# Half of an MLP's second product by seven block products instead of eight, interleaved with the next eighth's first product (fp32 decoder trunk, one core)

## The chip, the cores and the metric

The kernel runs on one core of a Trainium2 chip. The metric is the device time of one execution in microseconds; lower is better. A core has five engines with a queue each: TensorE (PE: matmuls, and the loads of the stationary operand, listed as PEld), VectorE (DVE), ScalarE (ACT), GpSimd (POOL) and SyncE (SP), which issues the loads from memory here. An engine takes the instructions of its queue in order, and waits for other engines by semaphores.

## The reference

Two layers on x of 256 tokens by 2048, in float32: a recurrent block (RG-LRU) and an attention block, each followed by an MLP, with RMS norms before each and one at the end. What matters here is the MLP:

```python
def _mlp(h, w1, w2):
    u = jnp.einsum('bsd,df->bsf', h, w1)      # 2048 -> 8192
    u = jnp.square(jax.nn.relu(u))
    return jnp.einsum('bsf,fd->bsd', u, w2)   # 8192 -> 2048
...
    x = x + _mlp(_rmsnorm(x, mlp_norm[i]), mlp_w1[i], mlp_w2[i])
```

## The kernel before

**Precision.** Every product of float32 numbers is made of three matmuls on rounded operands (type fp32r). A value v is split into hi, its rounding, and lo = v - hi; hi x hi, hi x lo and lo x hi are summed in PSUM, and lo x lo is left out. For weights ScalarE makes hi (`cut_hi`, L86) and VectorE makes lo (`cut_lo`, L90).

**Units.** All weights come in units of 128x2048 (1 MB). SyncE loads a unit into one of three `raw` tiles (L76); ScalarE writes `whi` (four tiles), VectorE `wlo` (three tiles); then TensorE uses both. `before_unit(i)` (L103) is called ahead of unit i's matmuls. It issues the loads up to unit i+5, hi up to i+3 and lo up to i+2. Instructions stand in each engine's queue in the order in which this code issues them. Functions that `after(n, ...)` puts off (evictions, sums) are issued behind the matmuls of the item n places later.

**A unit of the first product** (x W1) holds 128 columns of W1 over all 16 blocks of 128 inputs. Weights are stationary, x is moving: `xT` holds per input block 256 columns of hi and 256 of lo, one per token. Per block that is hi of the weights with x-hi and x-lo, and lo of the weights with x-hi: 768 columns. `stand_w2` (L252) issues them in an order named by a style. The three "thirds" styles (`thirds`, `thirds_low_first`) use three matmuls of 256 columns into one sum, 48 a unit. The others take hi over 512 columns at once, 32 matmuls a unit, and add the two halves later (`tensor_reduce`, L493). Each quarter of an MLP has its own style (L702, L709): `thirds`, `wide_first`, `pairs`, `apart` in the first MLP; `thirds_low_first`, `fours`, `thirds`, `as_was` in the second. `u_done` (L488) then makes relu, scaling and square, and splits the result into a tile `aT` of 128 hidden features by 256 tokens (hi and lo). It has one VectorE instruction or two on PSUM (L491, or L493 and L494), two on ScalarE (L496, L498) and one on VectorE (L502).

**A unit of the second product** holds 512 rows of W2 (four blocks of 128) by 512 output columns. Here `aT` is stationary, 128 tokens of it at a time, and the weights are moving. `stand_x` (L265) issues per block and per half t of the tokens three matmuls of 512 columns, 24 a unit, into two PSUM banks, one per half of the tokens.

**Order of the MLP** (`plan_mlp`, L504). There are four quarters of 2048 hidden features. Each quarter has 16 first units, then 16 second units: four output chunks n of 512 columns, four units each; then `add_x` (L290) adds the two banks to the residual `xc[n]` (L292). At the start of an MLP two first units are taken in two parts, since the last input chunk is still being transposed. The end of the second MLP is `final_items` (L671). It runs the last chunk's last three units for tokens 0 to 127 first, and then for tokens 128 to 255; `final_rows` (L654) normalises and stores each half.

**The other products** (L216 `stand_w` for the recurrent block, in the order hi, hi, lo of 256 columns each; `stand_x` for the rest) use the same units and buffers.

## Time and profile before

| | us |
|---|---|
| median of 3 runs | 2199.34 |
| lowest, highest | 2195.87, 2200.32 |
| the profiled execution's own time | 2199.65 |
| span in its profile (first to last instruction) | 2197.9 |
| TensorE busy | 2175.3 |
| VectorE busy | 1280.0 |
| ScalarE busy | 1061.3 |

The recurrent layer takes the first 384 us or so, the first MLP runs to 1094, the attention to 1483 and the second MLP to the end. The profile gives, per group of instructions, its line, engine, operation, the tiles that it writes and reads, its count, the busy time and the mean duration of one. The chain that ended last follows the end of the program back through what released each step. TensorE's durations overlap, since matmuls are pipelined, so its pace is read from the starts of matmuls. Where two rows of a timeline on VectorE or ScalarE overlap by some hundredths, the second began before the first had written its last result.

### The profile page before, as it was taken

To read this page: it belongs to the slowest core of one execution; us is meant where nothing else is said; L and a number is where in the kernel's file an instruction comes from. 1 tells how busy PE (TensorE), PEld (TensorE's weight loads), DVE (VectorE), ACT (ScalarE), POOL (GpSimd) and SP (SyncE) were. 2 spreads that over 40 slices of the span, in tenths; PEclk is the share of its full clock that TensorE was granted. 3 is DMA by queue.
4 is the path that set the end of the run, shared out by engine and by line. 5 is a ranking of instruction groups with operands and counts; after the bars stand their busy time and mean duration, and the time that the engine had idled before them with its cause. 6 is when DMAs were issued, how large, how long until landed. Compare 5 with 4: busy or idle time off the path is not lost.

```text
span 2197.9 us, 29494 instructions
## 1 busy us (share of the span) xinstructions
PE 2175.3 (99%) x12490; PEld 1910.4 (87%) x12490; DVE 1280.0 (58%) x1344; ACT 1061.3 (48%) x1163; POOL 78.3 (4%) x42
## 2 busy tenths in 40 slices
PE   7999999999999999999999999999999999999998
PEld 7999988998888888888888888889988889988886
DVE  8898855554564565565555555555546645545654
ACT  5787754543443343344445544555434434433442
POOL 2221100000000000000000000000000000000001
PEclk9999999999999999999999999999999999999999
DMA  6565555455555555555554445455555555555553
GB/s 219 211 211 194 194 207 189 175 192 191 191 183 201 185 188 197 189 189 194 181 192 166 159 174 183 161 188 199 200 195 181 198 196 184 186 193 189 191 192 115
DMA packets 61700, 413.40 MB, mean 188 GB/s; under 512 B 6784, under 2 KB 7168, under 8 KB 13440
## 3 DMA queue, kind: packets, MB, share of 16 engines
q1 hardware_dynamic: 61568, 411.51, 53.3%
q8 instruction: 98, 1.61, 0.3%
q14 instruction: 34, 0.28, 0.0%
HBM read 409.39 MB, written 2.10 MB: 187 GB/s over the span
## 4 chain that ended last, share of the span: by engine, by line
PE 96%; DVE 2%; ACT 1%; POOL 0%; DMA 0%; issue 0%; SPq 0%; DVEq 0%; ACTq 0%
PE acc L142 93%; PE g L142 1%; DVE wlo L90 1%; PE tr L176 0%; PE tr L568 0%; PE g L576 0%; DMA xg<-in_xT 0%; DVE xT L750 0%; PE tr L599 0%; POOL a L357 0%; ACT whi L86 0%; POOL c L358 0%; PE g L609 0%; PE g L608 0%; PE g L607 0%
## 5 line engine op out<-in xcount | busy, mean ns | idle before, releaser
L90 DVE TENSOR_TENSOR wlo<-raw,whi 128x2048 fp32r<-128x2048 f32 (+3 forms) x400 | 883.4, 2212 | 345.6 <-PE acc L142 267.9
L86 ACT ACTIVATE whi<-raw 128x2048 fp32r<-128x2048 f32 (+3 forms) x400 | 736.8, 1844 | 525.2 <-PE acc L142 437.6
L142 PE MATMUL acc<-xT,whi 128*128 128x256 f32 (+1 forms) x4064 | 882.7, 317 | 7.0 <-ACT whi L86 6.3
L142 PE MATMUL acc<-whi,aT 128*128 128x512 f32 x2624 | 813.9, 390 | 0.0
L142 PEld LDWEIGHTS acc<-xT,whi 128*128 128x128 f32 x4064 | 653.8, 190 | 46.4 <-ACT whi L86 6.7
L142 PE MATMUL acc<-xT,wlo 128*128 128x256 f32 x2672 | 654.9, 280 | 7.1 <-DVE wlo L90 6.8
L142 PEld LDWEIGHTS acc<-whi,aT 128*128 128x128 f32 x2624 | 492.6, 188 | 102.2
L142 PE MATMUL acc<-wlo,aT 128*128 128x512 f32 x1312 | 510.7, 389 | 0.0
L142 PEld LDWEIGHTS acc<-xT,wlo 128*128 128x128 f32 x2672 | 481.8, 190 | 27.6 <-DVE wlo L90 8.3
L142 PEld LDWEIGHTS acc<-wlo,aT 128*128 128x128 f32 x1312 | 246.3, 188 | 50.5
L142 PE MATMUL acc<-whi,xT 128*128 128x512 f32 x768 | 245.9, 395 | 0.0
L496 ACT ACTIVATE mu<-mr 128x256 f32<-128x256 f32 x128 | 53.5, 418 | 370.2 <-DVE mr L494 242.7
L142 PEld LDWEIGHTS acc<-whi,xT 128*128 128x128 f32 x768 | 144.3, 188 | 30.7
L142 PE MATMUL acc<-wlo,xT 128*128 128x512 f32 x384 | 150.4, 392 | 0.0
L493 DVE TENSOR_REDUCE mr<-acc 128x256 f32<-128x512 f32 x80 | 55.3, 692 | 156.1 <-PE acc L142 156.1
L292 DVE TENSOR_TENSOR xc<-xc,acc 128x512 f32<-128x512 f32 x78 | 53.2, 687 | 97.7 <-PE acc L142 97.7
L491 DVE SCALAR_TENSOR_TENSOR mr<-acc,rstdB 128x256 f32<-128x256 f32 x48 | 20.2, 424 | 112.9 <-PE acc L142 112.9
L142 PEld LDWEIGHTS acc<-wlo,xT 128*128 128x128 f32 x384 | 72.2, 188 | 15.1
L643 POOL TENSOR_TENSOR xc<-xc,gB 128x1024 f32<-128x1024 f32 x3 | 10.6, 3534 | 1879.9 <-DMA raw<-in_w 1843.4
L498 ACT ACTIVATE aT<-mu 128x256 fp32r<-128x256 f32 x128 | 53.6, 419 | 4.1
L502 DVE TENSOR_TENSOR aT<-mu,aT 128x256 fp32r<-128x256 f32 x128 | 53.4, 418 | 0.0
L189 ACT ACTIVATE junk<-xc 128x512 bf16<-128x512 f32 x32 | 20.2, 633 | 57.1 <-DVE xc L292 38.6
(143 smaller groups left out, 792.2 us busy)
## 6 DMA issues: line engine op xcount, KB each, us to landing
raw<-in_w SPq DMA_DIRECT2D x256, 1024.0 KB, 4.8
raw<-in_w_qkv SPq DMA_DIRECT2D x48, 1024.0 KB, 4.8
raw<-in_w_in SPq DMA_DIRECT2D x35, 1024.0 KB, 4.8
raw<-in_w_out SPq DMA_DIRECT2D x20, 1024.0 KB, 4.8
raw<-in_w_o SPq DMA_DIRECT2D x16, 1024.0 KB, 4.8
raw<-in_w_g SPq DMA_DIRECT2D x10, 512.0 KB, 3.3
raw<-in_w_in SPq DMA_DIRECT2D x11, 256.0 KB, 5.0
xc<-in_x SPq DMA_DIRECT2D x4, 512.0 KB, 5.7
```

The costliest lines, as they stand in the source:

```text
L86: nc.scalar.activation(split[i][0][:, s], r, AF.Copy)
L90: nc.vector.tensor_sub(split[i][1][:, s], r, split[i][0][:, s].bitcast(F32))
L142: nc.tensor.matmul(o, l, r, start=start, stop=stop, skip_group_check=True)
L189: nc.scalar.activation(junk, xc[n][:, t, :], AF.Square, accum_out=sq[:, t, n:n + 1])
L292: nc.vector.tensor_add(xc[n][:, t, :], xc[n][:, t, :], acc[t])
L491: nc.vector.scalar_tensor_tensor(r, ps[:, 0:256], 0.0, state["rstdB"], op0=OP.max, op1=OP.mult)
L493: nc.vector.tensor_reduce(r, ps.rearrange("p (b c) -> p c b", b=2), axis=AX.X, op=OP.add)
L496: nc.scalar.activation(uu, r, AF.Square)
L498: nc.scalar.activation(t[:, 0:256], uu, AF.Copy)
L502: nc.vector.tensor_sub(t[:, 256:512], uu, t[:, 0:256].bitcast(F32))
L643: nc.gpsimd.tensor_mul(xc[n], xc[n], state["gB"][:, None, n * 512:(n + 1) * 512].to_broadcast([P, NT, 512]))
```

## The change

An MLP is now planned in eighths p of 1024 hidden features (8 first units, and two second units, h = 0 and 1, for each of the four output chunks). Four things differ.

1. **Seven products.** In eighths 0 to 6 of both MLPs (`GROUPS`), the output chunks 0 and 1 together are a product of a 2x2 block matrix A (two halves of the tokens by two halves h of the eighth) with a 2x2 block matrix B (two halves h by two chunks). Before this took eight block products, four units of 24 matmuls. Now it takes seven block products by the Strassen-Winograd scheme (`plan_group`), each of 12 matmuls of 512 columns into one bank: on the blocks b11, b21 and b22 as they are, and on the sums t1 to t4. Sums of weight blocks are VectorE additions of 128x2048 (`add`, L564), written in place into the tiles `qT`, `q12`, `q21`, before the result is split like any unit. Sums of token blocks are made from `uu`, the squares kept in float32 (`sums_of_tokens`, four VectorE instructions of 128x128 for each of four blocks, then a split of 128x512 on ScalarE and VectorE into `sT`, L182). Each product is added to or subtracted from `xc` as it is done (`take`, L568). The four blocks are loaded once each, three of them into tiles of their own and b11 into a `raw` tile, which it keeps until its sum is made. Chunks 2 and 3, and all of eighth 7, stay with `stand_x` ("plain"), with `add_x` every two units instead of every four.

2. **Order.** The first units of the next eighth ("w") stand between the second units of this one, by the table `ORDER`, with "s" for a plain unit. I number the 19 places of a group from 0: b11 0, w 1, b21 2, s 3, w 4, t1 5, w 6, t2 7, b22 8, w 9, s 10, w 11, t3 12, w 13, s 14, w 15, t4 16, w 17, s 18; 0' is the next group's b11.

3. **First units** all go by `stand_w` (hi, hi, lo; 256 columns each), into the two `g` banks of PSUM; the styles and the `tensor_reduce` are gone.

4. **Buffers.** `whi` has three tiles instead of four, so hi of unit i+3 is issued behind the matmuls of unit i (`behind_unit`) and waits for their end. Transposes use the tiles q12 and q22 in place of `xg`. The memory set aside for DMA descriptors is cut from its default to 4096 bytes a partition. At the end of the second MLP the last chunk has two units instead of four, so the second half of the tokens is one part of 12 matmuls behind the first.

```diff
-HI_BUFS = 4
+HI_BUFS = 3
+SCRATCH = 4096
+GROUPS = range(7)
+ORDER = ("b11", "w", "b21", "s", "w", "t1", "w", "t2", "b22", "w", "s", "w", "t3", "w", "s", "w", "t4", "w", "s")
...
     def before_unit(i):
...
+        step("load", i + 1 + LOOK_LOAD, load)
+        step("make", i + LOOK_HI, make)
+        step("hi", i + LOOK_HI, cut_hi)
+        step("lo", i + 1 + LOOK_LO, cut_lo)
+
+    def behind_unit(i):
+        step("make", i + 1 + LOOK_HI, make)
+        step("hi", i + 1 + LOOK_HI, cut_hi)
...
+    def u_done(p, j, ps):
+        h, k = divmod(j, 4)
+        if h == 0:
+            squares[p, k] = lru.tile([P, 2, S], F32, name="uu", bufs=4)
+        uu = squares[p, k][:, h, :]
+        nc.vector.scalar_tensor_tensor(uu, ps[:, :S], 0.0, state["rstdB"], op0=OP.max, op1=OP.mult)
+        nc.scalar.activation(uu, uu, AF.Square)
+        t = new_aT(8 * (p % 2) + j)
         nc.scalar.activation(t[:, 0:256], uu, AF.Copy)
         after(1, u_low, t, uu)
+        if h == 1 and p in GROUPS:
+            after(1, waiting.append, (p, k))
...
+    def sums_of_tokens():
+
+        if not waiting or (busy[0] is not None and busy[0] < waiting[0][0]):
+            return
+        p, k = waiting.pop(0)
+        uu = squares.pop((p, k))
+        (a11, a21), (a12, a22) = ((uu[:, h, 0:128], uu[:, h, 128:256]) for h in range(2))
+        w = lru.tile([P, 4, 128], F32, name="sw")
+        nc.vector.tensor_sub(w[:, 0], a22, a21)
+        nc.vector.scalar_tensor_tensor(w[:, 1], w[:, 0], -1.0, a11, op0=OP.mult, op1=OP.subtract)
+        nc.vector.scalar_tensor_tensor(w[:, 2], w[:, 1], -1.0, a12, op0=OP.mult, op1=OP.subtract)
+        nc.vector.tensor_sub(w[:, 3], a11, a21)
+        t = lru.tile([P, 8, 128], F32R, name=f"sT{k}")
+        hilo(t[:, 0:4], t[:, 4:8], w)
+        state["sT", p, k] = t
...
+                    for k in range(4):
+                        xh, xl = get(k)
+                        s = slice(k * 512, (k + 1) * 512)
+                        mm(bank[b], xh, hi[:, s], first and k == 0, False)
+                        mm(bank[b], xh, lo[:, s], False, False)
+                        mm(bank[b], xl, hi[:, s], False, k == 3)
+                    for t in takes:
+                        after(0 if what == "a22" else 1, take, *t)
+                    if what == "s3":
+                        busy[0] = None
+                    if what == "a11":
+                        busy[0] = p
...
+                "b11": lambda: product([("b11", 0, 0, "raw")], [], "b11", "a11", "A", True, [(0, 0, "A", 1)]),
+                "b21": lambda: product([("q21", 1, 0, "q21")], [], "q21", "a12", "B", True, [(0, 0, "B", 1)]),
+                "t1": lambda: product([("q12", 0, 1, "q12")], [("qT", "b11", "q12")], "qT", "s0", "C", True,
+                                      [(1, 1, "C", -1)]),
+                "t2": lambda: product([("q22", 1, 1, "q22")], [("qT", "qT", "q22")], "qT", "s1", "A", False,
+                                      [(1, 0, "A", -1)]),
+                "b22": lambda: product([], [], "q22", "s2", "C", False, [(1, 0, "C", -1)]),
+                "t3": lambda: product([], [("q12", "q12", "q22")], "q12", "s3", "A", False, [(1, 1, "A", -1)]),
+                "t4": lambda: product([], [("q21", "q21", "qT")], "q21", "a22", "A", False, [(0, 1, "A", 1)]),
...
         part(0, range(NT))
         for t in range(NT):
-            for kq in (1, 2, 3):
-                part(kq, (t,))
+            part(1, (t,))
```

**TensorE, a block of a second unit before and a block product now.** Before, at the first second unit of the first MLP (chunk 0, hidden block 0: `aT0`), each block has six matmuls, three into the bank of each half of the tokens:

```order
L142 MATMUL acc_5376<-whi_5280,aT0_4120 128x512
L142 MATMUL acc_5376<-wlo_5312,aT0_4120 128x512
L142 MATMUL acc_5376<-whi_5280,aT0_4120 128x512
L142 MATMUL acc_5377<-whi_5280,aT0_4120 128x512
L142 MATMUL acc_5377<-wlo_5312,aT0_4120 128x512
L142 MATMUL acc_5377<-whi_5280,aT0_4120 128x512
```

Now, in the first MLP's group 1 at t4 (place 16; `tr_5305` is bank A, `whi_5844` and `wlo_5861` are t4's split), the end of the first unit at place 15 (bank `g_5904`) and the start of t4:

```order
L165 MATMUL g_5904<-xT3_4024,whi_5779 128x256 x2
L165 MATMUL g_5904<-xT3_4024,wlo_5792 128x256
L165 MATMUL tr_5305<-whi_5844,aT12_4713 128x512
L165 MATMUL tr_5305<-wlo_5861,aT12_4713 128x512
L165 MATMUL tr_5305<-whi_5844,aT12_4713 128x512
L165 MATMUL tr_5305<-whi_5844,aT13_4891 128x512
L165 MATMUL tr_5305<-wlo_5861,aT13_4891 128x512
```

A block product has three matmuls a block for four blocks, in one bank, and stands between two first units, where sixteen second units stood in a row.

**VectorE, the stretch ahead of a first unit.** Before, in the first MLP (`mr` holds the scaled relu of a first unit, `aT` gets its lo), each first unit has four instructions:

```order
L493 TENSOR_REDUCE mr_5580<-acc_5546 128x256
L494 SCALAR_TENSOR_TENSOR mr_5580<-mr_5580,rstdB_4114 128x256
L90 TENSOR_TENSOR wlo_5591<-raw_5462,whi_5542 128x2048
L502 TENSOR_TENSOR aT1_5585<-mu_5583,aT1_5585 128x256
L493 TENSOR_REDUCE mr_5627<-acc_5593 128x256
```

Now, in the first MLP's group 0, from the end of a sum of tokens (`sT1`) over the lo of t4 (`wlo_5082`) and the next sum of tokens (`sw`, `sT2`) to the lo of the first unit at place 17 (`wlo_5123`):

```order
L182 TENSOR_TENSOR sT1_5077<-sw_5072,sT1_5077 128x512
L106 TENSOR_TENSOR wlo_5082<-q21_4324,whi_5065 128x2048
L495 TENSOR_TENSOR aT14_5070<-uu_4979,aT14_5070 128x256
L505 TENSOR_TENSOR sw_5113<-uu_4979 128x128
L506 SCALAR_TENSOR_TENSOR sw_5113<-sw_5113,uu_4979 128x128
L507 SCALAR_TENSOR_TENSOR sw_5113<-sw_5113,uu_4979 128x128
L508 TENSOR_TENSOR sw_5113<-uu_4979 128x128
L182 TENSOR_TENSOR sT2_5118<-sw_5113,sT2_5118 128x512
L106 TENSOR_TENSOR wlo_5123<-raw_4984,whi_5110 128x2048
```

Ahead of these rows stand, in this order, the lo of place 15, the sum for t4 (L564), the take of t3 (L568), the eviction of place 13 (L486) and the four instructions of the sum of tokens that ends in `sT1`. The sums of the next eighth's tokens are held back until t3 has read the old ones (`busy`), so three of the four sets stand at places 12, 13 and 14, between the lo splits of places 14 to 17.

More of the change, by code (lines that the diff above doesn't have):

```diff
@@ L76, in load, with make @@
             nc.sync.dma_start(r[:, s], ap[:, s])
+    def make(i):
+        if "load" in units[i]:
+            units[i]["make"]()
+            raw[i] = [(slice(0, UW), units[i]["source"]())]
     def new_hi(i):
@@ L120, in trunk @@
     now = [0]
+    scope = [None]
     class Scope:
@@ L485, in plan_rec @@
                 oproj(n, kq)
-    def u_done(j, ps, style):
-        r = lru.tile([P, S], F32, name="mr", bufs=2)
-        if one_sum(style):
-            nc.vector.scalar_tensor_tensor(r, ps[:, 0:256], 0.0, state["rstdB"], op0=OP.max, op1=OP.mult)
-        else:
-            nc.vector.tensor_reduce(r, ps.rearrange("p (b c) -> p c b", b=2), axis=AX.X, op=OP.add)
-            nc.vector.scalar_tensor_tensor(r, r, 0.0, state["rstdB"], op0=OP.max, op1=OP.mult)
-        uu = lru.tile([P, S], F32, name="mu", bufs=2)
-        nc.scalar.activation(uu, r, AF.Square)
-        t = new_aT(j)
+    squares = {}
@@ L501, in u_low @@
     def u_low(t, uu):
         nc.vector.tensor_sub(t[:, 256:512], uu, t[:, 0:256].bitcast(F32))
-    def plan_mlp(w1, w2, done, styles):
-        for c in range(4):
-            us = []
-            def part(j, ks, first, last, us=us, c=c, style=styles[c]):
+    def sums_of_tokens():
+        if not waiting or (busy[0] is not None and busy[0] < waiting[0][0]):
+            return
+        p, k = waiting.pop(0)
[9 more added lines that the diff above has]
+        state["sT", p, k] = t
@@ L509, in run @@
                 def run():
                     if first:
-                        accs["u", j] = acc_tile()
-                    stand_w2(accs["u", j], us[j], ks, ks[0], first, last, style)
-                    if last:
-                        after(1 if c == 0 and j == 0 else 0, u_done, j, accs.pop(("u", j)), style)
-                item(us[j], run)
-            us.extend(unit(w1[c * 16 + j]) for j in range(16))
-            at = 0
-            if c == 0:
-                for j in range(2):
-                    part(j, range(0, 12), True, False)
-                for j in range(2):
-                    part(j, range(12, 16), False, True)
-                at = 2
@@ L525, in plan_mlp @@
-            for j in range(at, 16):
-                part(j, range(16), True, True)
-            for n in range(NCH):
-                last_c = c == 3
-                if last_c and n == NCH - 1 and done is final_done:
-                    final_items([unit(w2[(c * 4 + n) * 4 + kq]) for kq in range(4)])
-                    continue
-                for kq in range(4):
-                    u = unit(w2[(c * 4 + n) * 4 + kq])
-                    out_item(("m", n), u, aT, range(4 * kq, 4 * kq + 4), kq == 0, kq == 3,
-                             done(n) if last_c else (lambda acc, n=n: add_x(n, acc)))
+                        bank[b] = acc_tile() if b != "A" else psum.tile([P, 512], F32, name="tr", bufs=2)
@@ new lines, in plan_mlp @@
+        plan_start()
+        for j in (1, 5, 2, 6, 3, 7):
+            plan_first(0, j)
+        for p in range(8):
+            if p == 7 and done is final_done:
+                item(None, load_g)
+            if p < 7:
+                nxt = iter([(p + 1, j) for j in (0, 4, 1, 5, 2, 6, 3, 7)])
+            plain = [(n, h) for n in range(2 if p in GROUPS else 0, NCH) for h in range(2)]
+            g = plan_group(p, 0) if p in GROUPS else {}
+            for what in (ORDER if p in GROUPS else ("s", "w") * 8):
+                if what == "w":
+                    if p < 7:
+                        plan_first(*next(nxt))
+                elif what != "s":
+                    g[what]()
+                elif p == 7 and plain[0][0] == NCH - 1 and done is final_done:
+                    final_items([unit(w2[(12 + n) * 4 + 2 + h]) for n, h in plain])
+                    break
+                else:
+                    plan_plain(p, *plain.pop(0), p == 7)
@@ L790, in trunk @@
         cut_lo(i)
-    seen["load"], seen["hi"], seen["lo"] = 6, 6, 6
+    seen.update(load=6, make=6, hi=6, lo=6)
     acc3 = acc_tile()
@@ L815, in trunk @@
         later[6 + 2 * n] = [(load_x, (n,))]
-    for u, fn in items:
+    least = [len(units)] * (len(items) + 1)
+    for at in range(len(items) - 1, -1, -1):
+        u = items[at][0]
+        least[at] = least[at + 1] if u is None else min(u, least[at + 1])
+    least = least[1:]
+    for at, (u, fn) in enumerate(items):
         if u is None:
```

158 lines of the change are left out of this document (95 added, 63 removed).

## Prediction

> **What bounds the kernel now.** I read the page's engine line first, then the chain that ended last, then TensorE's waits after the start-up (from 84 us on), then two stages of the second MLP (a quarter's first product, then its second).
>
> ```profile
> PE 2175.3 (99%) x12490; PEld 1910.4 (87%) x12490; DVE 1280.0 (58%) x1344; ACT 1061.3 (48%) x1163; POOL 78.3 (4%) x42
> PE 96%; DVE 2%; ACT 1%; POOL 0%; DMA 0%; issue 0%; SPq 0%; DVEq 0%; ACTq 0%
> PE acc L142 <- DVE wlo L90: 2.6, 1, 2.6
> 1835.00:1924.00 89.00, 89.00 (x758) 89.00 (x757) 46.91 (x47) 41.25 (x46) 0.00 (x0) 1.00 0.52 182
> 1925.00:2011.00 86.00, 86.00 (x381) 71.22 (x380) 41.19 (x24) 31.49 (x18) 0.00 (x0) 1.00 0.56 192
> ```
>
> TensorE is busy 99% and is 96% of the chain. After 84 us it waited 2.6 us in all. In the MLP VectorE works 46.91 of 89 us and 41.19 of 86, ScalarE less, and the DMA engines are about half used. So the time is the number of matmuls times their pace, and work on other engines costs nothing until it comes too late for TensorE. The pace comes from the chain (start, length, count) and from TensorE's timeline:
>
> ```profile
> 130.09 21.78 PE acc L142 x192
> 396.56 635.72 PE acc L142 x3480
> 1495.56 693.86 PE acc L142 x4000
> 1747.39 0.39 PE L142 MATMUL acc<-whi,aT 128*128 128x512 f32 x1
> 1834.45 0.40 PE L142 MATMUL acc<-xT,whi 128*128 128x256 f32 x2
> 1924.90 0.39 PE L142 MATMUL acc<-whi,aT 128*128 128x512 f32 x1
> ```
>
> The last three rows begin a second product, a first product in the order hi, hi, lo (`thirds`) and the next second product. So 16 second units take 87.06 us: 5.441 a unit, 226.7 ns a matmul of 512 columns. And 16 first units take 90.45 us, 5.653 a unit. The first row is four units of the recurrent block, same order, same tile shapes: 21.78 us, 5.445 a unit. So one order of matmuls has two paces, 4% apart.
>
> **Part by part.** *Fewer matmuls.* Four units of 24 become seven products of 12: 12 matmuls fewer in each of 14 groups, 14 x 12 x 226.7 ns = **38.1 us** less, all on the path. I take 226.7 ns for the products too, the nearest row: same shapes, same widths.
>
> *The order of the first units.* In the row of 3480 matmuls 62 first units (14 x 48 + 48 x 32 = 2208) stand beside 53 second ones (1272): 635.72 - 53 x 5.441 = 347.4 us, 5.603 each. In the row of 4000 there are 62 first units (2464) and 64 second (1536): 345.6 us, 5.575 each. The mean over all styles is 5.589. After the change all 128 go hi, hi, lo: at the slow pace +128 x 0.064 = **+8.2 us**, at the fast one 128 x 0.144 = 18.4 us less. I take the slow one, because its row is the nearest: a first product that follows an MLP's second one, as every "w" will. The fast row follows the small gate matmuls of the recurrent block.
>
> *VectorE and ScalarE.* The durations come from the groups by shape, the spacing from VectorE's and ScalarE's timelines:
>
> ```profile
> L90 DVE TENSOR_TENSOR wlo<-raw,whi 128x2048 fp32r<-128x2048 f32 x112 | 256.1, 2287 | 103.0 <-PE acc L142 76.0 <-issue 26.9
> L86 ACT ACTIVATE whi<-raw 128x2048 fp32r<-128x2048 f32 x112 | 214.1, 1911 | 165.1 <-PE acc L142 144.0 <-DVE xc L292 21.1
> L292 DVE TENSOR_TENSOR xc<-xc,acc 128x512 f32<-128x512 f32 x24 | 16.4, 688 | 31.7 <-PE acc L142 31.7
> L491 DVE SCALAR_TENSOR_TENSOR mr<-acc,rstdB 128x256 f32<-128x256 f32 x16 | 6.7, 423 | 36.5 <-PE acc L142 36.5
> L159 DVE TENSOR_TENSOR xT<-xg,xT 128x512 fp32r<-128x512 f32 x24 | 15.5, 689 | 53.9 <-ACT xT L158 53.9
> L158 ACT ACTIVATE xT<-xg 128x512 fp32r<-128x512 f32 x24 | 14.0, 645 | 0.0
> L562 DVE TENSOR_TENSOR aq<-rw 128x128 f32<-128x128 f32 x8 | 2.3, 292 | 0.3
> 1834.65 1.92 ACT L86 ACTIVATE whi<-raw 128x2048 fp32r<-128x2048 f32 x1 [3.52 <-PE acc L142]
> 1840.30 0.42 DVE L491 SCALAR_TENSOR_TENSOR mr<-acc,rstdB 128x256 f32<-128x256 f32 x1 [2.77 <-PE acc L142]
> 1840.64 2.28 DVE L90 TENSOR_TENSOR wlo<-raw,whi 128x2048 fp32r<-128x2048 f32 x1
> 1842.84 0.42 DVE L502 TENSOR_TENSOR aT<-mu,aT 128x256 fp32r<-128x256 f32 x1
> 1840.76 0.42 ACT L496 ACTIVATE mu<-mr 128x256 f32<-128x256 f32 x1 [4.20 <-DVE mr L491]
> ```
>
> Spacing is 0.08 us below duration where nothing is waited for (1840.64 + 2.28 against 1842.84): 2.20 for a lo, 0.34 for an eviction or `aT`, 0.61 for a take. A weight sum is not in the trace; it has a lo's shape and operation, so 2.20. ScalarE starts 0.2 us after TensorE's next unit (1834.65 against 1834.45), and 0.04 us after VectorE (1840.72 to 1840.76). Of a token sum's four 128x128 instructions two are like the 0.292 row; the other two lie between 0.292 and the 0.423 of twice the size. I take 1.2 us for the four; the upper end is 1.43.
>
> VectorE's work per group is then 19 lo 41.8, 4 sums 8.8, 8 evictions and `aT` 5.4, 11 takes and adds 6.7, 4 token sums 7.2: 70 us. TensorE's is 8 x 5.65 + 4 x 5.44 + 7 x 2.72 = 86 us. VectorE fits on the whole, at 81%, but a queue in order can still be late at one place. I walked the 19 places by hand. Everywhere but one the lo is ready 1 us or more ahead. The exception is the first unit at place 17, behind t4.
>
> Take the end of place 11 as 0. Hi of place 14 starts at 0.2 and ends at 2.1, its lo begins at 2.15. From there VectorE has three lo (14, 15, t4) 6.6, the sum for t4 2.2, a take 0.6, an eviction 0.34, two `aT` 0.67, three token sums 3.6, their three lo 1.8 and the lo of place 17 2.29. It also waits for ScalarE: 0.7, 1.25 and 0.7 us between each token sum and its lo. (In the second, ScalarE first makes hi of t4 and two squares; behind these waits stand the lo that TensorE needs.) With three hops of 0.05 the sum is 23.1 us. TensorE meanwhile has places 12 to 16, 2.72 + 5.65 + 5.44 + 5.65 + 2.72 = 22.2 us, and two matmuls (0.23) ahead of the first that needs lo: 22.4. It waits 0.7 us, with a hop 0.8: 14 x 0.8 = **+11 us**. Bounds: none, if the chain is 0.8 us shorter; 0.7 more with token sums at 1.43, and 0.7 more with no overlap between instructions, 2.2 a group or 31 us.
>
> The Trainium skill (VectorE: DVE Perf Modes, The DRAIN you can't avoid) says that the next VectorE instruction does not start until the pipe has emptied. Here it starts 0.08 us before the former's end, so the trace does not agree for these pairs. By the rule the chain would have eight spacings of 0.08 more, 14 x 0.67 = 9 us, and the sum would be 2192.
>
> *Loads.* Bytes are the same. b11 holds one of three `raw` tiles until t1's sum, and the load of place 1' waits for the lo of place 17:
>
> ```profile
> raw<-in_w SPq DMA_DIRECT2D x256, 1024.0 KB, 4.8
> ```
>
> It is issued at 23.1 and lands at 28; its hi is due at the end of place 17, 28.7, its lo 8 us later. Behind it in SyncE's queue stand q21' and the load of 3', due more than 8 us later. I count nothing; without that cover, each would cost its lateness up to 4.8 us.
>
> *Hi one unit later* (three `whi` tiles): it is issued at the end of unit i for unit i+3, with at least 5.4 us for 1.9. Nothing. The vanished `tensor_reduce` was off the path. Nothing.
>
> *The tail.* VectorE's rows for the two halves of the tokens:
>
> ```profile
> 2181.29 0.69 DVE L656 TENSOR_TENSOR xc<-xc,acc 128x512 f32<-128x512 f32 x1 [5.76 <-PE acc L142]
> 2184.48 1.92 DVE L668 TENSOR_SCALAR xc<-xc,fs 128x512 f32<-128x512 f32 x4
> 2189.45 0.69 DVE L656 TENSOR_TENSOR xc<-xc,acc 128x512 f32<-128x512 f32 x1 [3.05 <-PE acc L142]
> ```
>
> The first half's closing work takes 2181.29 to 2186.40, 5.1 us, under 8.2 us of matmuls. Now 2.72 us of matmuls lie over it, and the second half's add stands behind it in VectorE's queue: **+2.4 us**.
>
> Sum, on the profiled execution's own 2199.65 (0.3 above the median): - 38.1 + 8.2 + 11 + 2.4 = 2183.2, so **2183**.
>
> **Rivals.** *The fast pace.* The first units settle at 5.445, as in the recurrent block; part of the second MLP's first quarter, in another order, had it too. For it: one order shows both paces, so the pace hangs on how the stretch is entered, and it is now entered 8 times a group. Against it: the entry at 1834.45. TensorE would reach place 17 0.4 us sooner and wait 1.2 us a group: 2199.65 - 38.1 - 18.4 + 17 + 2.4 = 2163. Chance 0.22.
>
> The Trainium skill (TensorE: Matmul & The Clock Gate, Wait — 56ns, not 53.3ns?) gives start to start as the columns at 2.4 GHz plus 2.5 ns, 109 ns for 256, with no second pace. No row here is that fast (21.78 us / 192 = 113 ns), but it would favour this case.
>
> *VectorE decides (the other side).* The stretch from place 12 to 17 is longer than I make it, through the token sums and their three round trips to ScalarE, and TensorE waits for the lo of place 17 (then of others) in every group. It is no gain from 1.6 us a group on (2199.65 - 38.1 + 8.2 + 2.4 + 14 x 1.6 = 2194.6) and a loss from 2.3 on, a chain of 24.6 us; 3 us a group would give 2214. For it: 20 instructions in one queue, four kinds of them without a row. Against it: the slack of a us or more at the other places. Chance 0.13, 0.05 of it within 0.2%.
>
> *Late loads.* With b11 in a `raw` tile two tiles serve the rest. If one load a group comes 2.6 us late to its unit, 14 x 2.6 = 36 us are lost: 2219. Against it: the walk leaves 4 us or more. Chance 0.05, 0.02 of it within 0.2%.
>
> **How the numbers follow.** The forecast has 0.60, from 2172 (no wait) to 2194.6 (1.6 us a group). A measurement here can tell about 0.2% from no change (the three runs lie 4.4 us apart), so faster means under 2194.9. Faster: 0.60 + 0.22 = 0.82; within 0.2%: 0.05 + 0.02 = 0.07; slower: 0.08 + 0.03 = 0.11. The range goes from 2160 (the fast pace; below it a tenth, where there is no wait as well) to 2204.
>
> **What would show it.** TensorE's matmul records should fall by 168 for the products, and rise by 16 for each of the units that had 32. First units should start 5.65 us apart (5.45: the fast pace). TensorE's waits should name `wlo` about once a group, some 0.8 us each, at the unit behind t4. VectorE should be busy near 80% in the MLPs. Waits of over 2 us a group, at several places, or for loads, would make the prediction wrong; so would matmuls of 512 columns off 227 ns in the products.

## The result, and the profile after

The changed kernel takes 2186.39 us (median of 4 runs, 2186.15 to 2188.10), the kernel before 2198.90 us (median of 4): ratio 0.9947, 95% interval 0.9929 to 0.9964. The profiled execution took 2186.37 us, 13.3 us less than that of before.

The engine line, the start of the chain's shares, and TensorE's waits after 84 us (us in total, times, longest) of the changed kernel:

```profile
PE 2150.0 (98%) x13602; PEld 1944.2 (89%) x13602; DVE 1602.2 (73%) x1748; ACT 1166.2 (53%) x1261; POOL 81.3 (4%) x42
PE 80%; DVE 12%; ACT 5%; issue 2%; POOL 0%; DMA 0%; SPq 0%; DVEq 0%; ACTq 0%
```
```profile
PE g L165 <- DVE uu L486: 5.8, 2, 2.9
PE acc L165 <- DVE wlo L106: 4.2, 7, 2.4
PE g L165 <- DVE wlo L106: 2.1, 12, 0.2
```

TensorE still bounds the kernel: it is busy 98% of the span. But its share of the chain fell from 96% to 80%; ahead of place 17 and in the recurrent layer the chain now runs through VectorE and ScalarE. VectorE went from 58% to 73%, and to 78% in each MLP (near 80% was forecast). The matmul count moved as foreseen: 16 more in each of 80 units that had 32, 168 fewer in the products, 12490 + 1280 - 168 = 13602. The third kind of wait is the one the prediction spoke of. The first kind, and six of the seven waits of the second, it did not foresee. (The 2.4 us one is the end of the start-up, 2.6 us before.)

By stage, from the start of a stage's first matmul to that of the next (the tail from the start of the last matmul), in the two profiled executions:

```
us                 before   after
recurrent layer    384.14   388.95    +4.8
first MLP          710.53   698.52   -12.0
attention          388.33   388.64    +0.3
second MLP         706.02   697.14    -8.9
tail                 8.85    11.33    +2.5
                                     -13.3
```

The pace, from TensorE's timeline in a group (start, length, what): a first unit begins, the product behind it begins, the next first unit begins.

```profile
453.61 0.28 PE L165 MATMUL g<-xT,whi 128*128 128x256 f32 x1
...
459.26 0.39 PE L165 MATMUL acc<-whi,sT 128*128 128x512 f32 x1
...
461.98 0.40 PE L165 MATMUL g<-xT,whi 128*128 128x256 f32 x2
```

The unit takes 5.65 us (117.8 ns a matmul), the product 2.72 us (226.7 ns): both as forecast. All 100 first units of the groups that do not wait take 5.65 us.

Place 17. VectorE's rows from the end of place 11 (576.12) on, the first and the last of the walk's terms, and the three waits for ScalarE:

```profile
578.15 2.29 DVE L106 TENSOR_TENSOR wlo<-raw,whi 128x2048 fp32r<-128x2048 f32 x1 [1.41 <-ACT whi L102]
...
582.53 0.69 DVE L182 TENSOR_TENSOR sT<-sw,sT 128x512 fp32r<-128x512 f32 x1 [0.70 <-ACT sT L181]
583.14 2.28 DVE L106 TENSOR_TENSOR wlo<-raw,whi 128x2048 fp32r<-128x2048 f32 x1
585.35 2.28 DVE L564 TENSOR_TENSOR q<-q,qT 128x2048 f32<-128x2048 f32 x1
...
590.95 0.69 DVE L182 TENSOR_TENSOR sT<-sw,sT 128x512 fp32r<-128x512 f32 x1 [1.34 <-ACT sT L181]
...
595.93 0.69 DVE L182 TENSOR_TENSOR sT<-sw,sT 128x512 fp32r<-128x512 f32 x1 [0.70 <-ACT sT L181]
596.54 2.28 DVE L106 TENSOR_TENSOR wlo<-raw,whi 128x2048 fp32r<-128x2048 f32 x1
```

and TensorE's at place 17:

```profile
598.30 0.40 PE L165 MATMUL g<-xT,whi 128*128 128x256 f32 x2
598.88 0.38 PE L165 MATMUL g<-xT,wlo 128*128 128x256 f32 x1 [0.18 <-DVE wlo L106]
599.10 0.40 PE L165 MATMUL g<-xT,whi 128*128 128x256 f32 x2
```

The lo is done at 598.82, 22.7 us after the end of place 11 (walk: 23.1), and was due at 598.30 + 0.235 = 598.54. From 598.30 the third matmul starts 0.34 us late; the next interval, 598.88 to 599.10, is 0.1 us too long as well. That is 0.44 us, in 12 of 14 groups. But in nine of the twelve the rest of the unit then goes at 113.3 ns: the unit takes 5.91 us, only 0.26 more than its neighbours. All twelve cost 9 x 0.26 + 3 x 0.44 = 3.7 us.

The start of the first MLP, which the prediction did not walk: TensorE, ScalarE and VectorE.

```profile
404.29 0.50 PE L165 MATMUL g<-xT,whi 128*128 128x256 f32 x2 [2.91 <-DVE uu L486]
```
```profile
399.66 3.71 ACT L102 ACTIVATE whi<-raw 128x2048 fp32r<-128x2048 f32 x2 [1.30 <-PE g L165]
403.28 0.36 ACT L241 ACTIVATE rstdB<-tr 128x256 f32<-128x256 f32 x1
```
```profile
401.61 2.29 DVE L106 TENSOR_TENSOR wlo<-raw,whi 128x2048 fp32r<-128x2048 f32 x1 [2.27 <-ACT whi L102]
403.81 0.75 DVE L486 SCALAR_TENSOR_TENSOR uu<-g,rstdB 128x256 f32<-128x256 f32 x2
```

First units now sum in two `g` banks, where four `acc` banks served before. The first two units are evicted only when rstdB is there, and ScalarE makes rstdB behind two hi and VectorE the evictions behind a lo. So the third unit has no bank for 2.9 us, in each MLP.

The recurrent layer: the chain of waits over one block (start, us, what), shortened in its middle.

```profile
203.17 2.15 PE g L165 x19
205.32 0.31 ACT aT L181
205.63 0.53 ACT gw L368
...
209.21 0.06 DVE c L349
209.28 0.34 issue
209.61 2.29 DVE wlo L106
211.91 0.04 issue
211.95 2.11 PE acc L165 x16
```

In the kernel before this stretch is TensorE alone. Now it leaves TensorE for ScalarE's aT and gw, which in ScalarE's queue stand behind a hi, then for VectorE's chain up to a lo that comes 0.3 us late. One block comes every 25.17 us where it came every 24.58.

The tail, VectorE's add for the second half of the tokens, with no idle time before it:

```profile
2174.14 1.91 DVE L764 TENSOR_SCALAR xc<-xc,fs 128x512 f32<-128x512 f32 x4
2175.98 0.68 DVE L752 TENSOR_TENSOR xc<-xc,acc 128x512 f32<-128x512 f32 x1
```

It queues behind the first half's closing work, as forecast (+2.4; measured +2.5).

### The profile page after: what moved, and what is told of

Its sections match the earlier page's. It is cut to its first block, busy times and chain, and to the rows that moved or that the text cites. A ratio compares the mean times of both kernels' runs of the same rounds, so it can differ in the third digit from the quotient of the medians.

```text
span 2184.6 us, 32102 instructions
## 1 busy us (share of the span) xinstructions
PE 2150.0 (98%) x13602; PEld 1944.2 (89%) x13602; DVE 1602.2 (73%) x1748; ACT 1166.2 (53%) x1261; POOL 81.3 (4%) x42
## 4 chain that ended last, share of the span: by engine, by line
PE 80%; DVE 12%; ACT 5%; issue 2%; POOL 0%; DMA 0%; SPq 0%; DVEq 0%; ACTq 0%
PE acc L165 47%; PE g L165 27%; DVE wlo L106 7%; PE tr L165 4%; ACT whi L102 3%; DVE q L564 1%; ACT sT L181 1%; DVE xT L843 0%; DVE c L349 0%; DVE sT L182 0%; PE tr L205 0%; DVE aT L495 0%; DVE sw L506 0%; PE tr L664 0%; PE g L672 0%
## 5 line engine op out<-in xcount | busy, mean ns | idle before, releaser
L165 PE MATMUL g<-xT,whi 128*128 128x256 f32 x4128 | 732.9, 281 | 5.8 <-DVE uu L486 5.8
L165 PEld LDWEIGHTS g<-xT,whi 128*128 128x128 f32 x4128 | 638.0, 188 | 15.2 <-DVE uu L486 6.3
L165 PE MATMUL g<-xT,wlo 128*128 128x256 f32 x2064 | 580.4, 281 | 2.1 <-DVE wlo L106 2.1
L165 PE MATMUL acc<-whi,aT 128*128 128x512 f32 x1840 | 580.5, 390 | 0.0
L165 PEld LDWEIGHTS g<-xT,wlo 128*128 128x128 f32 x2064 | 395.3, 192 | 4.6 <-DVE wlo L106 4.6
L165 PE MATMUL acc<-wlo,aT 128*128 128x512 f32 x920 | 358.3, 389 | 0.0
L165 PE MATMUL acc<-xT,whi 128*128 128x256 f32 x1248 | 223.5, 283 | 6.3 <-ACT whi L102 5.8
L165 PEld LDWEIGHTS acc<-xT,whi 128*128 128x128 f32 x1248 | 195.0, 194 | 6.9 <-ACT whi L102 6.1
L165 PE MATMUL acc<-xT,wlo 128*128 128x256 f32 x624 | 178.2, 286 | 9.3 <-DVE wlo L106 9.0
L165 PEld LDWEIGHTS acc<-xT,wlo 128*128 128x128 f32 x624 | 121.0, 194 | 12.0 <-DVE wlo L106 12.0
```

Of the source, the lines that this page charges most:

```text
L165: nc.tensor.matmul(o, l, r, start=start, stop=stop, skip_group_check=True)
```

## The experiments

Each is compared by its ratio to runs of the kernel before on the same chip (medians 2196.4 to 2198.7 us); the changed kernel's own ratio is 0.9947. Sizes under 5 us are read from stages of the profiled executions. The time up to the first gate matmul differs between runs of one kind (49.5 to 55.4 us); it is left out where the recurrent layer is compared.

### The recurrent layer: three `whi` tiles alone

```
 HI_BUFS = 3                                   # in the kernel before
     before_unit(u)                            # hi up to u + LOOK_HI - 1
     fn()
+    behind_unit(least[at] - 1)                # hi up to LOOK_HI units ahead
     for f, args in later.pop(now[0], []):
```

> The kernel before with one part of the change alone: three whi tiles in place of four, and hi of unit i+3 issued behind unit i. Theory (the recurrent layer got longer because hi, issued a unit later, stands ahead of ScalarE's aT and gw there and so delays VectorE's queue up to wlo): the recurrent layer takes 388 to 389 us in place of 384.1, the MLPs and the attention change by under 1 us, and the whole takes 2203 to 2204 us, 4.8 us more than before. Rival (the recurrent layer's loss comes from the smaller DMA scratch or from where the tiles lie, which this kernel leaves as before): no change, 2199 us.

Measured: 2205.56 us, ratio 1.0032 (1.0020 to 1.0043). From the first gate matmul to the first MLP it takes 335.2 us; before 330.2, the changed kernel 335.2. Both MLPs are as before (710.53 and 706.02 us). The chain has the same steps:

```profile
206.94 0.31 ACT aT L163
207.25 0.53 ACT gw L384
...
211.24 2.29 DVE wlo L90
```

So three `whi` tiles, and hi issued behind the unit, alone make the whole of this loss. The scratch and the layout, which this kernel leaves alone, have no part in it.

### The recurrent layer: hi behind the work that falls due

```
+        if scope[0] != "rec":
             behind_unit(least[at] - 1)
         for f, args in later.pop(now[0], []):
             f(*args)
+        behind_unit(least[at] - 1)
```

> The changed kernel with hi of unit i+3, in the recurrent layer alone, issued behind the work that falls due at the end of unit i (aT, gw, gates and the rest), not ahead of it. Theory (the recurrent layer is 4.8 us longer because hi stands ahead of those activations in ScalarE's queue): from the first gate matmul on it takes 330 to 331 us as in the kernel before, not 335 to 338, and the whole takes 2181 to 2182 us. Rival (three whi tiles make the layer longer whatever the order, since hi cannot start before unit i is done and wlo of unit i+3 comes late for it): 335 us or more there, 2186 us or more in all, with TensorE waiting for wlo or whi.

Measured: 2190.18 us, ratio 0.9961 (0.9949 to 0.9974): a miss as a whole, 337.7 us from the first gate on. (With the changed kernel's order of hi this stretch took 335.2 to 337.9 us in the nine traces that have it; the kernel before took 330.2.) The periods between the blocks' gates tell why:

```
before            19.22 29.35 24.58 24.58 24.58 24.58 24.58 24.58 24.59
changed           19.23 29.39 25.17 25.17 25.17 25.17 25.17 25.78 25.17
three whi alone   19.62 27.76 25.77 25.15 25.77 25.15 25.16 25.78 25.17
hi behind         25.63 27.66 27.36 24.58 24.58 24.58 24.58 24.58 24.60
```

From the fourth period on the blocks come every 24.58 us: in the steady state the order of ScalarE's queue is the whole cause. In the first three periods the same order is bad. There hi has no lead yet, and it now stands behind the gates' sigmoids and table loads; VectorE stands idle for it:

```profile
68.32 2.29 DVE L106 TENSOR_TENSOR wlo<-raw,whi 128x2048 fp32r<-128x2048 f32 x1 [5.30 <-ACT whi L102]
```

### No products at all

```
-GROUPS = range(7)
+GROUPS = range(0)
```

> The changed kernel with no group by seven products (all of the second product in plain units; eighths, tiles and the hi, hi, lo order stay). Theory (the 168 matmuls saved are all on the path at 226.7 ns, and what VectorE's extra work gives back is only the wait at place 17, 0.27 us a group): 38.1 us more and 3.8 us less, 2186.4 + 34.3 = 2220.7 us, first units at 5.65 us. Rival (the extra work on VectorE and ScalarE gives back more than the wait at place 17, spread over other places): under 2212 us.

Measured: 2220.23 us, ratio 1.0102 (1.0087 to 1.0116). The two MLPs are 35.5 us longer than in the changed kernel (38.1 - 3.7 would be 34.4; 1.2 us of the 35.5 lies at the starts of the MLPs, in the pace of six units and a stretch at half the clock), and all first units behind 512-column matmuls take 5.65 us here too. The product scheme alone is worth some 35 us; the rest of the change gives about 22 us back.

### VectorE's queue ahead of place 17

```
         nc.vector.tensor_sub(w[:, 0], a22, a21)
+        nc.vector.scalar_tensor_tensor(w[:, 1], w[:, 0], -1.0, a11, op0=OP.mult, op1=OP.subtract)
+        nc.vector.scalar_tensor_tensor(w[:, 2], w[:, 1], -1.0, a12, op0=OP.mult, op1=OP.subtract)
+        nc.vector.tensor_sub(w[:, 3], a11, a21)
+        nc.vector.tensor_sub(w[:, 0], a22, a21)
```

> The changed kernel with the four VectorE instructions of a token sum issued twice, to the same results: 1.15 us more of VectorE at each, three of them between places 12 and 17. Theory (VectorE's queue from place 12 to the lo of place 17 is what TensorE waits for, and it has no slack): 3.4 us more wait in each of 14 groups, 48 us, 2234 us, all of it at place 17 for wlo. Rival (VectorE's work lies beside TensorE's with slack, and the 0.27 us of wait at place 17 come from something else, such as ScalarE's hi): under 2195 us.

Measured: 2222.29 us, ratio 1.0109 (1.0091 to 1.0126). The MLPs are 41.6 us longer. TensorE's waits in the MLPs:

```profile
PE g L165 <- DVE wlo L106: 32.6, 12, 2.7
PE g L165 <- DVE uu L486: 5.8, 2, 2.9
```

At each of the same twelve places the third matmul now starts 3.00 us after the second, where it was 0.455: 2.54 us more, 30.5 us in all. The place and the sign hold, and there is no slack to speak of. The work added is 1.06 us for each of three sums, 3.18, and in the second sum the wait for ScalarE falls from 1.34 to 0.70 us, since ScalarE now has its squares done when the sum comes; 3.18 - 0.64 = 2.54:

```profile
595.52 0.69 DVE L182 TENSOR_TENSOR sT<-sw,sT 128x512 fp32r<-128x512 f32 x1 [0.70 <-ACT sT L181]
```

Most of the other 11 us is no wait. Behind six of the twelve gaps, and behind the wait at the start of the first MLP, the clock records show 3.41 us at 0.50 of the clock, and the unit takes about 1.5 us longer for it (9.89 to 10.15 us, where 8.44 to 8.64 follow the other six gaps).

### The last two places exchanged

```
-ORDER = ("b11", "w", "b21", "s", "w", "t1", "w", "t2", "b22", "w", "s", "w", "t3", "w", "s", "w", "t4", "w", "s")
+ORDER = ("b11", "w", "b21", "s", "w", "t1", "w", "t2", "b22", "w", "s", "w", "t3", "w", "s", "w", "t4", "s", "w")
```

> The changed kernel with the last two places of a group exchanged: the plain unit directly behind t4, the eighth first unit last. Theory (the wait is that of the first unit at place 17, whose lo is due 0.2 us into it; a plain unit needs its lo as early, but the work queued ahead of it is the same, so what counts is that the deadline of the eighth unit moves): if the wait belongs to the queue ahead of place 17 whatever stands there, it stays at 0.27 us, now at the plain unit, 2186 us. If it belongs to the first unit alone (its raw tile, its load), it goes: 3.7 us less, 2182.7 us.

Measured: 2191.93 us, ratio 0.9967 (0.9955 to 0.9980). The wait stays, now at the plain unit, twelve times 0.2 us by the waits view:

```profile
PE acc L165 <- DVE wlo L106: 2.2, 12, 0.2
```

But the MLPs are 5.1 us longer than in the changed kernel, not the same. A plain unit with the wait takes 5.95 us where it takes 5.44: 0.51 lost, where the first unit mostly lost 0.26. The lateness is the same; a plain unit has no second pace to win back 0.2 us by. That makes 12 x 0.51 - 3.7 = 2.4 us; the rest is at the starts of the MLPs, where five first units went at the slow pace and the third unit of the first took 1.6 us longer, at half the clock for 3.41 us.

### The start of an MLP in `acc` banks

```
-                accs["u", 0, j] = psum.tile([P, 512], F32, name="g", bufs=2)
+                accs["u", 0, j] = acc_tile()              # in plan_start
```

> The changed kernel with the first two units of each MLP summed in acc banks in place of the two g banks. Theory (the third first unit waits 2.9 us at the start of each MLP because both g banks are held until the evictions that wait for rstdB): 5.8 us less, 2180.6 us, and no wait of a third unit for uu. Rival (the two evictions are late whatever the bank, and the third unit or the next waits for something else, wlo or rstdB's own bank): 2186.4 us.

Measured: 2178.42 us, ratio 0.9909 (0.9896 to 0.9923). The waits for uu are gone, and the MLPs are 2.3 and 4.9 us shorter, 7.2 in all. The two differ from 2.9 by what the wait had done to the matmuls behind it. The chain has six first units there, 288 matmuls, in the changed kernel and in this one; the first MLP is the first row of each, the second MLP the second:

```profile
404.29 32.93 PE g L165 x288
1491.60 34.52 PE g L165 x288
```
```profile
400.49 33.92 PE g L165 x288
1485.54 32.66 PE g L165 x288
```

In the first MLP the six had gone at 113.4 ns behind the wait and now go at 117.8: 1 us of the 2.9 is given back. In the second they go at 113.4 in both, but behind the wait 16 matmuls had gone at half the clock. The stretches of the changed kernel (length, PE and PEld, DVE, ACT, POOL, PEclk, DMA share, GB/s), before the wait, within it, behind it, later:

```profile
1484.00:1488.00 4.00, 4.00 (x36) 4.00 (x36) 1.62 (x8) 3.52 (x7) 0.00 (x0) 1.00 0.18 74
1488.50:1491.50 3.00, 0.18 (x2) 0.00 (x0) 2.58 (x3) 2.45 (x3) 0.00 (x0) 1.00 0.00 0
1492.20:1495.30 3.10, 3.10 (x16) 3.10 (x16) 2.54 (x3) 0.96 (x3) 0.00 (x0) 0.50 0.96 336
1496.00:1500.00 4.00, 4.00 (x37) 4.00 (x36) 0.98 (x4) 1.16 (x1) 0.00 (x0) 1.00 0.56 231
```

16 matmuls at 0.50 of the clock are 1.6 us more: with 2.9 of wait and some smaller parts, the 4.9. The like wait in the first MLP did not lower the clock. The Trainium skill (TensorE: Matmul & The Clock Gate, Why this matters for your kernels) advises against gaps of TensorE above about 3 us, since one window of idleness brings half the clock. The traces agree with it only in part. The gaps here are 2.9 us of idleness (3.19 from start to start), and one of the two lowered the clock. So did both in the kernel with another order, below (2.6 us, 2.83 and 2.84 from start to start), and six of twelve in the kernel with the token sums twice (2.7 us, 3.00 from start to start). So gaps under 3 us aren't safe here.

### The pace: another order within the unit

```
+        todo = ([(hi, j, k, 0) for j, k in enumerate(ks)] + [(hi, j, k, 256) for j, k in enumerate(ks)]
+                + [(lo, j, k, 0) for j, k in enumerate(ks)])
```

> The changed kernel with the 48 matmuls of a first unit of an MLP in another order: 16 hi by x hi, 16 hi by x lo, then 16 lo by x hi, all still 256 columns. Theory A (the slow pace of 117.8 ns belongs to hi, hi, lo in turn; one kind after another goes at 113.4 ns): first units take 5.44 us, 128 x 0.21 = 27 us less, and lo is due 3.6 us later, so the wait at place 17 goes too (3.8 us): 2156 us. Theory B (the slow pace comes from entering a 256-column unit out of 512-column matmuls, whatever the order): first units stay at 5.65 us and only the wait goes: 2182.6 us.

Measured: 2182.63 us, ratio 0.9928 (0.9915 to 0.9942). The time is theory B's, but in part by accident: the MLPs are only 1.7 us shorter, the rest lies in the recurrent layer's start. All 112 units of the groups take 5.65 us, so the order hi, hi, lo is not the cause. The wait at place 17 is gone (3.7 us less). At the starts of the MLPs 2 us are lost again: five units of the second went slow that had been fast, and the third unit of the first had matmuls at half the clock (behind a gap of 2.83 us; that of the second MLP had them too, as in the changed kernel).

### The pace: a transpose ahead of the unit

```
                 accs["u", p, j] = psum.tile([P, 512], F32, name="g", bufs=2)
+                nc.tensor.transpose(accs["u", p, j][:, 256:384], ident, ident)
```

> The changed kernel with one transpose of 128 columns (into the unused half of the bank, read by nobody) ahead of each first unit that stands between 512-column matmuls. By the trace of the changed kernel two such transposes take 0.13 us and the unit behind them 0.1 us more, so I put 0.17 us on each of 124 units. Theory A (entering the unit directly from 512-column matmuls sets the slow pace; other matmuls between leave it to chance): half of the units at 5.44 us, 124 x (0.17 - 0.105) = 8 us more, 2194 us, a mixture of 5.44 and 5.65 in the trace. Theory B (a 512-column stretch before sets the slow pace whatever stands between): all at 5.65, 21 us more, 2207 us. Theory C (any other matmul between resets to the fast pace): all at 5.44, 5 us less, 2181 us.

Measured: 2185.69 us, ratio 0.9939 (0.9924 to 0.9954): theory C in the groups, but not elsewhere. Of the 100 units in the groups that have only the transpose between them and 512-column matmuls, and do not wait, 99 go at 113.3 ns, 5.57 us with the transpose; one, the first of the second MLP's groups, goes at 117.8. At the start of each MLP five units with their transpose follow another first unit, and four of the five go at 117.8. So a transpose doesn't reset anything; it changes the entry, one way here and the other way there. A gain of 99 x 0.08 = 8 us is given back: 4.6 at those starts (with half the clock in the first MLP as well), the rest at place 17 (units of 6.01 us and more there) and in the 512-column stretches behind the faster units.

### The pace: side by side

```
+                if p == 3:
+                    mm(accs["u", p, j][:, 256:257], ident, ident[:, 0:1], True, True)
...
+            mm(ps[:, 0:n], hi[:, s], x[:, 0:n], first and j == 0, False)      # n = 128, 64, 32 for p = 1, 2, 6
+            mm(ps[:, n:256], hi[:, s], x[:, n:256], first and j == 0, False)
```

> The changed kernel with another first matmul ahead of the first units, a different one for each eighth p, in both MLPs, so that one trace shows them side by side (14 to 16 units each). p = 1, 2, 6: the unit's own first matmul in two pieces, 128 + 128, 64 + 192, 32 + 224 columns (no column more). p = 3: a plain-float32 matmul of 1 column into the unused half of the bank, p = 4: an fp32r one of 128 columns, p = 5: a plain-float32 one of 64 columns; nobody reads them. p = 7: nothing, as in the changed kernel. Theory A (any narrower matmul between the 512-column stretch and the unit resets the pace): all but p = 7 go at 113.4 ns a matmul, about 5.44 to 5.54 us a unit. Theory B (the plain-float32 type of the transposes reset it, not their width): p = 3 and 5 at 5.44 to 5.54, p = 1, 2, 4, 6 and 7 at 5.65 and more. Theory C (what resets it is a short gap at the head of the unit, 0.1 us, whatever makes it): the fast units are those whose second matmul starts late. By theory A about 80 units gain 0.1 to 0.2 us: 2170 to 2178 us; by B, 32 units, 2181 to 2186 us.

For p = 1, 2 and 6 the second piece begins the sum anew, so the first piece's share is left out of the result; the matmuls issued are those told. Measured: 2186.72 us, ratio 0.9948 (0.9931 to 0.9964). Each form gives one pace, the same in all of its units that do not wait, in both MLPs:

```
p   ahead of, or at the head of, the unit    us a unit   ns a matmul
7   nothing                                    5.65        117.8
1   pieces 128 + 128                           5.56        113.3
6   pieces 32 + 224                            5.57        113.3
2   pieces 64 + 192                            5.76        117.8
3   float32, 1 column                          5.67        113.3
5   float32, 64 columns                        5.67        113.3
4   fp32r, 128 columns                         5.76        117.8
```

From the timeline, one unit of p = 1, one of p = 2 and one of p = 7, its first row and the first behind it:

```profile
453.47 0.50 PE L165 MATMUL g<-xT,whi 128*128 128x128 f32 x3
...
459.03 0.39 PE L165 MATMUL acc<-whi,sT 128*128 128x512 f32 x1
...
539.57 0.50 PE L165 MATMUL g<-xT,whi 128*128 128x64 f32 x3
...
545.33 0.40 PE L165 MATMUL acc<-whi,sT 128*128 128x512 f32 x1
...
972.17 0.40 PE L165 MATMUL g<-xT,whi 128*128 128x256 f32 x2
...
977.83 0.39 PE L165 MATMUL acc<-whi,sT 128*128 128x512 f32 x1
```

Theory A falls by p = 2 and 4. Theory B falls by p = 1 and 6. Theory C falls too: every form that is not p = 7 has a late matmul near its head.

### The three repairs together

```
+        if scope[0] != "rec" or u < 14:                    # hi first only up to unit 13
             behind_unit(least[at] - 1)
...
+        behind_unit(least[at] - 1)
-                accs["u", 0, j] = psum.tile([P, 512], F32, name="g", bufs=2)
+                accs["u", 0, j] = acc_tile()
-        part(0, range(NT))
         for t in range(NT):
+            part(0, (t,))
             part(1, (t,))
```

> The changed kernel with three edits in three separate stages. Recurrent layer, from its 14th unit on: hi of unit i+3 behind the work due at the end of unit i. Start of each MLP: the first two units in acc banks. End: both units of the last plain chunk for the first half of the tokens, then both for the second half, so that 24 matmuls (5.4 us) lie over the first half's closing work of 5.1 us. Theory: the blocks of the recurrent layer come every 24.58 us from the third gate on, not 25.17 (7 x 0.59 = 4.1 us less); 2 x 2.9 us less at the starts of the MLPs; the time behind the last matmul's start 8.9 us, not 11.3 (2.5 us less): 2186.4 - 12.4 = 2174 us. Rivals: the recurrent layer's switch of order costs a transition of 2 to 3 us, as its start did when it held from the first unit (2177 us); the second half of the tokens waits for its bank or its lo and the tail gains nothing (2176.5 us).

Measured: 2172.78 us, ratio 0.9883 (0.9869 to 0.9898). The periods are 19.62, 29.33, then 24.58 seven times: the switch costs nothing. From the first gate on the recurrent layer takes 330.6 us (changed kernel 335.2; 330.2 and 330.7 in the two kernels below, which keep this edit). The MLPs are 2.1 and 4.8 us shorter, the tail 9.05 us (11.33). The chain over the block shown above is TensorE alone again:

```profile
199.95 1.13 PE acc L165 x10
201.08 2.80 PE g L165 x24
203.88 10.22 PE acc L165 x90
```

### Pieces at other places, and the version that beats both

Both on top of the three repairs; a pair gives which matmul of the unit is cut, from 0, and at which column. The sum begins once, with the first piece.

```
+                ent[0] = {1: (1, 128), 2: (0, 160), 3: (0, 96), 4: (0, 16), 5: (2, 128), 6: (0, 224), 7: (0, 128)}.get(p)
```

> The kernel with the three edits (2172.8 us), and in each first unit of the groups one of its 48 matmuls cut in two pieces, no column more, another cut for each eighth p: p = 1: the second matmul 128 + 128; p = 2: the first 160 + 96; p = 3: the first 96 + 160; p = 4: the first 16 + 240; p = 5: the third 128 + 128; p = 6: the first 224 + 32; p = 7: the first 128 + 128. The run with the cuts of the changed kernel showed 128 + 128 and 32 + 224 at the head going at 113.3 ns (5.56 us a unit) and 64 + 192 at 117.8 (5.76). Theory (two paces, each of which holds itself; the phase at which the stretch is entered chooses, so a cut chooses by its place and not by its being there): p = 7 at 113.3 ns again, the others split between the two paces, each p the same in all of its units; about half fast, 2172.8 - 56 x 0.09 + 56 x 0.1 = 2173 us. Rival (any cut near the middle resets the pace, a small or late one does not): p = 1, 2, 3, 5 and 7 fast, 4 and 6 slow, 80 x 0.09 - 32 x 0.1 = 4 us less, 2169 us.

Measured: 2175.28 us, ratio 0.9901 (0.9884 to 0.9917). The pieces 128 + 128 go at 113.3 ns wherever they stand (first matmul 5.56 us a unit, second 5.58, third 5.59); 160 + 96, 96 + 160, 16 + 240 and 224 + 32 stay at 117.8 (5.76). A cut as such does nothing; which cut it is, decides, and the same in every unit without a wait. The rival falls, since 160 + 96 and 96 + 160 stay slow; the theory holds in kind, each p with one pace, but that a phase is the reason isn't shown by it. Then that cut in all 112 units:

```
+                ent[0] = (0, 128) if p else None
```

> The kernel with the three edits (2172.8 us), and the first matmul of each of the 112 first units in the groups cut 128 + 128. Theory (the cut sets the fast pace: 5.56 us a unit and not 5.65; TensorE comes to place 17 two units, so 0.18 us, sooner and waits that much longer, since VectorE's queue sets the time there): 112 x 0.09 - 14 x 0.18 = 7.6 us less, 2165 us. Rival (the groups are already bound by VectorE and ScalarE at more places than 17, so the faster units are given back as waits): 2171 to 2173 us.

Measured: 2164.75 us, ratio 0.9856 (0.9840 to 0.9873), 0.9% under the changed kernel. The 100 units that do not wait take 5.56 us. All 112 are 7.6 us shorter than in the kernel with the three edits, as the theory has it, but the 512-column stretches behind them are 1.5 us longer, so the MLPs gain 6.1 us; the other 2 us between the two kernels' times lie ahead of the first MLP, where they do not differ. Those at place 17 take 6.05 to 6.26: VectorE's queue sets their time, and TensorE only comes there sooner. Its waits after 84 us:

```profile
PE g L165 <- DVE wlo L106: 2.6, 12, 0.2
```

## Why the prediction was right, and where it was not

*Fewer matmuls: right.* 168 fewer, each 226.7 ns in the products too; 38.1 us. Without the products the MLPs are 35.5 us longer.

*The order of the first units: right in its value, by a poor reason.* With the other terms as measured, the MLPs' change of -20.9 us leaves -20.9 + 38.1 - 3.7 - 5.8 = +7.7 for it (forecast +8.2); the half clock's 1.6 us is part of this, as is a gain of some 2 us from ten or so fast units. The nearest row was the right one: a unit entered from 512-column matmuls is slow, in each of 100 cases. But order has no part in it, as the kernel with another order showed. The rival's argument, that being entered eight times a group would bring the fast pace by chance, fails: straight from 512-column matmuls the pace is the same each time.

*VectorE's queue: right in place, mis-sized.* Forecast 0.8 us a group, 11 us. Measured 0.44 us of delay, of which 0.2 is won back in most cases, and in twelve groups, not fourteen: eighth 7 stays plain, so in the last group of each MLP no token sums stand in the queue. That is 3.7 us in all. The chain was 22.7 us, not 23.1; no single term is far off, and the waits for ScalarE were 0.70, 1.34, 0.70 against 0.7, 1.25, 0.7. That the queue has no slack, which is what the rival of the other side rested on, held: 3.18 us more of work, less 0.64 of waiting for ScalarE, made 2.54 us more of wait at each place. The time of 2192 by the rule of the emptying pipe rests on half of what its section states: the Trainium skill (VectorE: DVE Perf Modes, The DRAIN you can't avoid) adds that a next instruction that is not held starts earlier, and that is what the rows above show (595.93 + 0.69 against 596.54).

*"Hi one unit later ... Nothing": wrong, +4.8 us.* I weighed hi's own due time (5.4 us for 1.9) and not what stands behind it in ScalarE's queue. In the recurrent layer aT and gw do, and VectorE's chain to the next lo hangs on them. Three tiles alone made the loss; the other order of ScalarE's queue took it away.

*The start of the MLPs: not walked at all, +5.8 us.* The sums of the first units moved from four banks to two, and there the banks are held longest, until rstdB. Other banks took the wait away, and with it 7.2 us.

*Late loads, the vanished `tensor_reduce`: nothing*, as forecast; no wait names either. *The tail: right*, +2.5 against +2.4, and 2.3 of it came back when both units of the last chunk stood behind each other for each half of the tokens.

So two unseen losses, 10.6 us, stand against a wait that was put 7.3 us too high. The total was 3.4 us off because these largely cancel, not because each step held.

## What to carry to other kernels

When a change takes a buffer away, walk not only the buffer's own due time but every instruction that stands behind the later one in the same queue, and do it in each stage that shares the helper. A change within a loop also moves its edges: look at the first two iterations and at the banks that they hold. When a product alone saves 35 us and 13 arrive, the difference sits in named places, and small repairs there (here an order of a queue, two banks, the order of the last units, one cut) brought some 20 us more, by the ratios.

## What the runs showed of the hardware

A run of 256-column matmuls has two paces here, 113.3 and 117.8 ns, both at a granted clock of 1.00, and holds the one it starts in. Coming straight from 512-column matmuls it was 117.8 in every unit without a wait; with the first, second or third matmul cut 128 + 128 it was 113.3 in every unit without one; cuts at 16, 64, 96, 160 and 224 gave 117.8, a cut at 32 gave 113.3. A wait within the unit can change it as well: at place 17 nine units of twelve went on at 113.3 ns. Behind the wait at the start of the first MLP the units went at 113.3 in the changed kernel and at 117.8 in the kernel with the entries side by side, which has the same instructions there; so there the pace isn't set by the order of instructions alone. A transpose ahead gave 113.3 in 99 of 100 units behind 512-column matmuls, and 117.8 in eight of ten behind 256-column ones. That the phase at which the stream is entered decides would fit all of this, but it was not tested, and what in the chip would have that phase is open; no record of the trace shows it.

A wait of 0.34 us for an operand costs 0.44 us: the interval behind the late matmul was 0.22 us where 0.12 is usual, at all twelve places.

A gap in TensorE's work of about 3 us, from start to start of matmuls, was followed in some cases, and not in others, by 3.41 us at 0.50 of the clock, in which the matmuls of 256 columns took 1.4 to 1.6 us longer. Of gaps of 3.19 us (the starts of the MLPs in seven kernels) ten of fourteen did it, of 2.98 to 3.00 us (the token sums twice) six of twelve, of 2.83 and 2.84 us (another order) both. The two MLPs of one kernel can differ in it, so a time read over one such gap has up to 1.6 us of luck in it.
